# Three hand-overs between engines in a two-layer encoder step: weight low parts to VectorE, output scaling to ScalarE and GpSimd, one chunk normalised tile by tile

## The chip, the cores and the metric

The kernel runs on one core of a Trainium2 chip. A core has five engines that run their own instruction streams in order: TensorE (PE; its weight loads are shown apart as PEld), VectorE (DVE), ScalarE (ACT), GpSimd (POOL) and SyncE (SP), whose queue issues nearly all DMAs here. They wait for one another by semaphores. The metric is device microseconds of one execution, the median over the timed runs. The profile is one more execution, recorded by the hardware profiler.

## The reference, cut to what matters

The reference is one inference step of a two-layer encoder: 2048 prompt frames and one chunk of 64 sample frames with caches, model width 1024, all in fp32. Each layer is

```python
xn = _rms(h, pre_g)
...                                   # projections of xn @ w_in, gated attention of the layer
return h + _rms((o * jax.nn.silu(g)) @ w_out, post_g), state

def _rms(x, g):
    y = xf * lax.rsqrt(jnp.mean(xf * xf, axis=-1, keepdims=True) + RMS_EPS)
    return (y * g).astype(x.dtype)
```

Layer 0 has two groups of heads (latent attention over all earlier chunks, and a band of nine chunks with a learned bias), layer 1 a sliding window of three chunks with grouped queries (16 query heads, 2 key heads) and attention sinks. The new cache rows are outputs too.

## The kernel before, in words

All matrix products are made to fp32 accuracy out of fp32r products: an operand is split into a high part (fp32 rounded to fp32r by a copy on ScalarE) and a low part (the fp32 value minus the high part), and three products of high and low parts are added up in PSUM (`mm3`, L231). So nearly every operand costs a copy on ScalarE and a subtraction on another engine. Tiles that come out of PSUM get their low part on DVE (`lo_of`, L213); a few that lie in SBUF get it on POOL: the projection weights (`load_w`, L228), the gated attention output (L1749 in phase 5, L1268 in phase 3).

The work stands in five phases. In the trace, phase 1 (projections of layer 0) runs to about 715 us, phase 2 (latent attention) to about 1345, phase 3 (band attention and layer 0's W_out) to about 1850, phase 4 (projections of layer 1) from about 1805 to 2270, and phase 5 (window attention and layer 1's W_out) from there to the end.

*Weights and inputs (phases 1 and 4).* `load_w` (L216) brings a block of projection columns in pieces of up to 1024 columns: a DMA into a raw buffer R, the high part by ScalarE (L227), the low part by POOL (L228). `norm_chunk` (L243) brings up to three tiles of 128 tokens into the same raw buffers (there are five in phase 1), squares and sums each on ScalarE (L255), makes the reciprocal root of the mean on DVE by three Newton steps of tiny operations (`rstd_of`, L180: for the three tiles together, 128x3, unless `start` is given, as it is for the very first chunk, where each tile has its own chain on 128x1), scales the tile by it and by the row of gains (L263), and transposes it on PE (L267) into X. A 128x1 chain takes three DVE operations for a Newton step (L195 to L197), a 128x3 chain four (L192, L193, L196, L197).

*W_out and its tail (phases 3 and 5).* `out_proj` (L966) multiplies the split MM of 128 tokens with W_out in two halves of 512 columns, evicts them to z, and sums their squares on ScalarE (L982). Its `tail` then makes the reciprocal root on POOL and DVE, scales z by it and by the gains on DVE (L994, two halves of 512), adds the residual x on POOL (L1002) and sends the rows out. The very last tile (`J.last`) does all on DVE and in halves.

*Phase 5's steady part.* A block is 128 queries and 4 units (2 key heads by 2 parities). A unit scores on PE (L1684), adds the mask and takes maxima on DVE (L1687, L1688), adds the sink on POOL (L1689), exponentiates on ScalarE (L1696), sums on POOL (L1700), turns on PE (L1705) and splits P into PT (L211 on ScalarE, L214 on DVE), multiplies with V on PE (L1712), and writes its part of OT on DVE (L1802). OT has two buffers, taken in turn. After four units the `gate` (L1714) scales OT by the sums (L1736), multiplies it with the gate G on POOL (L1742), and splits it into MM (high L211 on ScalarE, low L1749 on POOL), which is free for W_out afterwards. W_out's products and tails of earlier blocks are spread between these steps by a pump.

*What sets the order.* A scheduler of the framework orders the instructions of each engine by simulated times. In phase 3 and in phase 5 after the first steps it is switched off for PE, DVE, ScalarE and SP: there the order is that in which the code issues. POOL's order is the scheduler's throughout.

Of the kernel before, what the change touches and what calls it, by code (L numbers as in the profile page):

```python
# [10 lines left out]
AF = mybir.ActivationFunctionType  # L11
ALU = mybir.AluOpType
# [4 lines left out]
SEQ, DS, PAST, DM = 2048, 64, 1024, 1024  # L17
# [45 lines left out]
HALVES4 = [HALVES[1], HALVES[0]]  # L63
# [47 lines left out]
def kernel(ctx, tc, a, o, upto=5):  # L111

    nc = tc.nc
    S = K()
    dma = nc.sync.dma_start
# [25 lines left out]
    sH = scratch("sH", [T, 1024])  # L141
# [74 lines left out]
    def load_w(pw, raw, src, kt, w, slot):  # L216

        W = pw.tile([128, slot], F32R, name="W")
        Wv = W[:, :2 * kt * w].rearrange("p (a k c) -> p a k c", a=2, k=kt)
        sv = src.rearrange("(k p) c -> p k c", p=128)  # L220
        step = max(1, 1024 // w)
        for k0 in range(0, kt, step):
            k1 = min(kt, k0 + step)
            R = raw.tile([128, 1024], F32, name="R")
            Rv = R[:, :(k1 - k0) * w].rearrange("p (k c) -> p k c", c=w)
            dma(Rv, sv[:, k0:k1])
            nc.scalar.activation(Wv[:, 0, k0:k1], Rv, AF.Copy)  # L227
            nc.gpsimd.tensor_tensor(Wv[:, 1, k0:k1], Rv, Wv[:, 0, k0:k1], op=ALU.subtract)  # L228
        return Wv

    def mm3(ps, lhs, rhs, kt):  # L231
# [8 lines left out]
    def prompt_or_sample(t0, r):  # L240
        return a["x_prompt"][t0:t0 + r] if t0 < SEQ else a["x_sample"]

    def norm_chunk(px, raw, xin, pt, src, g_pre, c0, n, start=None):  # L243

        X = px.tile([128, 2, KT, 384], F32R, name="X")
        tiles = tok_tiles(c0, n)
        ss = xin.tile([128, 3], F32, name="ss3")
        if tiles[-1][2] < 128:
            nc.gpsimd.memset(ss, 1.0)
        xs = []  # L250
        for i, (t0, off, r) in enumerate(tiles):
            x = raw.tile([128, 1024], F32, name="R")
            dma(x[:r], src(t0, r))
            sq = xin.tile([128, DM], mybir.dt.bfloat16, name="sq", bufs=1)
            nc.scalar.activation(sq[:r], x[:r], AF.Square, accum_out=ss[:r, i:i + 1])  # L255
            xs.append(x)
            if start and i == 0:
                start()
        y = None if start else rstd_of(ss[:, :len(tiles)], 128, DM)
        for i, (t0, off, r) in enumerate(tiles):  # L260
            x = xs[i]
            yi = rstd_of(ss[:, i:i + 1], 128, DM) if start else y[:, i:i + 1]
            nc.vector.scalar_tensor_tensor(x[:r], x[:r], yi[:r], g_pre[:r], op0=ALU.mult, op1=ALU.mult)  # L263
            for k0 in range(0, KT, 4):
                p = pt.tile([128, 4, 128], F32, name="pt")
                for k in range(4):
                    nc.tensor.transpose(p[:, k, :r], x[:r, (k0 + k) * 128:(k0 + k + 1) * 128], ident[:r, :r])  # L267
                hi = X[:, 0, k0:k0 + 4, off:off + r]
                copy(hi, p[:, :, :r])
                lo_of(X[:, 1, k0:k0 + 4, off:off + r], p[:, :, :r], hi)  # L270
        return X
# [694 lines left out]
    def out_proj(J, wk, zp, M, W, t0, r, res, g_post, put):  # L966
# [3 lines left out]
        z = z0 or zp.tile([128, DM], F32, name="z", bufs=2)  # L970
        ss = small.tile([128, 2], F32, name="ss2")
# [12 lines left out]
        def tail():  # L984
            eng = nc.vector if J.last else nc.gpsimd
            eng.tensor_tensor(ss[:r, 0:1], ss[:r, 0:1], ss[:r, 1:2], op=ALU.add)
            y = rstd_of(ss[:r, 0:1], r, DM, eng)
            if not J.last:
                yield
                yield  # L990
                yield
            for c in range(2):
                cs = slice(c * 512, c * 512 + 512)
                nc.vector.scalar_tensor_tensor(z[:r, cs], z[:r, cs], y, g_post[:r, cs], op0=ALU.mult, op1=ALU.mult)  # L994
                if J.last:
                    eng.tensor_tensor(res[:r, cs], z[:r, cs], res[:r, cs], op=ALU.add)
                    dma(put(t0, r)[:, cs], res[:r, cs])
                elif c == 0:
                    yield
            if J.last:  # L1000
                return
            nc.gpsimd.tensor_tensor(res[:r], z[:r], res[:r], op=ALU.add)  # L1002
            for _ in range(1 + DPUT):
                yield
            J.put(put(t0, r), res[:r])
# [30 lines left out]
    def jobs(banks):  # L1036
        J = K()
        J.loaded, J.ready, J.made, J.done, J.banks, J.n, J.credit = False, [], 0, 0, banks, 0, 0.0
        J.last, J.put = False, dma
        J.early, J.half, J.n_early, J.MM = [], {}, 0, {}  # L1040
        J.side, J.tails, J.load, J.samp = Fill(), Fill(), Fill(), Fill()

# [418 lines left out]
    def phase4():  # L1461

        with ExitStack() as st, ExitStack() as st_m:
            pool, pool_m = pools(st, "left"), pools(st_m, "left")
            px0, pw0 = pool("px4", 1), pool("pw4", 1)
            raw, rows, xin = pool_m("raw4", 6), pool_m("rows4", 1), pool_m("xin4", 2)
            px, pw = Ring(px0), Ring(pw0)
# [72 lines left out]
            Xs4 = {}  # L1540

            def build(c):
                Xs4[c] = norm_chunk(px, raw, xin, pt, lambda t0, r: sH[t0:t0 + r], g_pre, *c)

            def weights(col, specs):
                w = 256 if specs == ["kv"] else 128 * len(specs)
# [28 lines left out]
                            yield  # L1575
                put()

            build(HALVES4[0][0])
            W = weights(*pieces[0][0])
            yield  # L1580
            keep = ctx.enter_context(tc.tile_pool(name="keep", bufs=1, side="right", reuse_waits="tile"))
# [64 lines left out]
    def phase5():  # L1646

        with ExitStack() as st:
# [4 lines left out]
            ps_o, ps_p = pool("ps_o5", 1, space=PSUM), pool("ps_p5", 1, space=PSUM)  # L1653
            J = jobs([(ps_p, "proj")])
            J.open = 0
            J.mm = None
            mask = one.tile([128, 256], F32, name="mask")
            nc.gpsimd.memset(mask, 0.0)
            nc.gpsimd.memset(mask[0:64, 192:256], NEG)
# [366 lines left out]
```

## Time and profile before

| what | value |
|---|---|
| three timed runs | 2733.17, 2735.3, 2743.01 us; median 2735.3 |
| the profiled execution | 2728.45 us, its span 2726.7, mean granted TensorE clock 0.985 |
| PE / PEld busy | 94% / 86% of the span |
| DVE / ACT / POOL busy | 54% / 51% / 28% |
| DMA | 437.92 MB, 161 GB/s over the span |

Lines of the timeline and of the groups give the start, the duration in us, engine, line, operation, out<-in and shapes; behind them, in brackets, the idle time of the engine just ahead and who ended it. A row with x2 or more stands for several instructions that follow each other. Lines of waits give the total in us, the number of times, and the longest.

### The profile page before, as it was taken

What the parts mean: (1) busy time and instruction counts of PE and PEld (TensorE: products, weight loads), DVE (VectorE), ACT (ScalarE), POOL (GpSimd) and SP (SyncE); (2) the same over time, 40 slices, a digit from 0 to 9 for tenths busy, and PEclk for the clock granted to TensorE, in tenths of its full rate; (3) what the DMA queues carried; (4) which work ended last, traced back from release to release, by engine and by line L of the source; (5) the groups of instructions that cost most, each with busy time, mean ns of one, the idle gap of its engine ahead of it and who ended that gap; (6) DMA issues with size and microseconds to landing.
All of it is one profiled execution on the core that took longest, in us unless ns stands there. A gap on an engine that the chain in (4) does not pass through costs nothing.

```text
span 2726.7 us, 46699 instructions
## 1 busy us (share of the span) xinstructions
PE 2565.9 (94%) x16296; PEld 2340.5 (86%) x16296; DVE 1471.5 (54%) x4050; ACT 1392.1 (51%) x3548; POOL 772.6 (28%) x1312
## 2 busy tenths in 40 slices
PE   6999999999999999999999999989999999999997
PEld 6999999899998888888777878769999998787886
DVE  5542235352127878787667666545113104787884
ACT  4332232333237777777666665552233224777783
POOL 2123122113112323321101323553113220344444
PEclk9999999999999999999899999999999999999999
DMA  6456443737537666661477676756525429455551
GB/s 236 160 155 213 124 150 97 249 110 228 165 95 210 183 180 188 170 165 55 169 202 187 179 187 172 205 187 216 155 99 166 128 70 250 109 139 134 136 132 70
DMA packets 382283, 437.92 MB, mean 161 GB/s; under 512 B 49937, under 2 KB 308889, under 8 KB 378817
## 3 DMA queue, kind: packets, MB, share of 16 engines
q1 hardware_dynamic: 382048, 434.95, 54.4%
q8 instruction: 129, 2.11, 0.3%
q14 instruction: 106, 0.86, 0.1%
HBM read 282.80 MB, written 157.09 MB: 161 GB/s over the span
## 4 chain that ended last, share of the span: by engine, by line
PE 73%; DVE 10%; ACT 6%; DMA 5%; issue 3%; POOL 2%; SPq 0%; ACTq 0%; DVEq 0%; POOLq 0%
PE pm L237 37%; PE proj L963 10%; PE s L682 6%; PE acc L753 4%; PE t L725 3%; DVE PT L214 2%; PE acc L1215 2%; PE t L1705 2%; PE acc L1712 2%; PE s L1175 2%; PE t L1202 1%; PE s L1684 1%; ACT P L701 1%; DVE m L688 1%; ACT PT L211 1%
## 5 line engine op out<-in xcount | busy, mean ns | idle before, releaser
L237 PE MATMUL pm<-X,W 128*128 128x384 f32 (+2 forms) x4536 | 753.4, 325 | 2.4 <-DVE ev L214 0.9
L237 PEld LDWEIGHTS pm<-X,W 128*128 128x128 f32 x4536 | 732.5, 190 | 5.5 <-DVE ev L214 1.1
L211 ACT ACTIVATE PT<-t 128x512 fp32r<-128x512 f32 (+3 forms) x704 | 344.6, 505 | 272.0 <-PE t L1202 120.4
L214 DVE SCALAR_TENSOR_TENSOR PT<-t,PT 128x512 fp32r<-128x512 f32 (+3 forms) x688 | 375.5, 569 | 105.2 <-ACT PT L211 103.4
L963 PE MATMUL proj<-Wo,MM 128*128 128x512 f32 (+1 forms) x1464 | 404.0, 406 | 18.1 <-ACT z L211 14.7
L228 POOL TENSOR_TENSOR W<-R,W 128x768 fp32r<-128x768 f32 (+3 forms) x114 | 230.4, 2048 | 534.0 <-ACT W L227 533.7
L214 DVE SCALAR_TENSOR_TENSOR ev<-pm,ev 128x256 fp32r<-128x256 f32 (+3 forms) x197 | 98.7, 503 | 467.3 <-ACT ev L1552 169.3
L963 PEld LDWEIGHTS proj<-Wo,MM 128*128 128x128 f32 (+1 forms) x1464 | 252.2, 186 | 68.8 <-ACT z L211 20.1
L237 PE MATMUL pm<-W,X 128*128 128x256 f32 (+5 forms) x2040 | 281.2, 297 | 0.0
L237 PEld LDWEIGHTS pm<-W,X 128*128 128x128 f32 (+1 forms) x2040 | 271.6, 187 | 1.4 <-POOL W L228 0.3
L701 ACT ACTIVATE P<-s,m 128x512 f32<-128x512 f32 (+9 forms) x344 | 209.5, 616 | 32.8 <-DVE m L690 30.5
L682 PE MATMUL s<-KA,Q 128*128 128x512 f32 (+7 forms) x640 | 201.1, 396 | 9.7 <-ACT P L701 8.8
L725 PE MATMUL t<-ident,P 128*128 128x128 f32 x1088 | 176.3, 276 | 3.4 <-ACT P L701 0.8
L688 DVE TENSOR_REDUCE m<-s 128x1 f32<-128x480 f32 (+7 forms) x216 | 132.4, 613 | 79.1 <-PE s L682 78.7
L725 PEld LDWEIGHTS t<-ident,P 128*128 128x128 f32 x1088 | 134.7, 141 | 41.5 <-ACT P L701 14.9
L753 PE MATMUL acc<-PT,V 128*128 128x256 f32 x1152 | 155.9, 285 | 6.6 <-DVE OT L762 6.6
L753 PEld LDWEIGHTS acc<-PT,V 128*128 128x128 f32 x1152 | 140.3, 188 | 12.0 <-PE t L725 6.0
L1696 ACT ACTIVATE P<-s,m 128x256 f32<-128x256 f32 (+2 forms) x264 | 119.7, 466 | 11.6 <-DVE m L1688 10.3
L1687 DVE CUSTOM_DVE_ANT_0 s<-s,mask 128x256 f32<-128x256 f32 (+1 forms) x256 | 107.7, 422 | 19.0 <-PE t L1705 8.1
L682 PE MATMUL s<-KR,Q 128*128 128x384 f32 (+6 forms) x320 | 116.3, 363 | 0.7 <-DMA Q<-sQR 0.7
L227 ACT ACTIVATE W<-R 128x768 fp32r<-128x768 f32 (+3 forms) x114 | 98.2, 910 | 36.5 <-DMA R<-in_ab_w_in_dram 18.2
L1179 DVE CUSTOM_DVE_ANT_0 s<-s,bias 128x640 f32<-128x640 f32 (+4 forms) x128 | 95.2, 744 | 38.6 <-PE s L1175 37.3
(249 smaller groups left out, 3961.0 us busy)
## 6 DMA issues: line engine op xcount, KB each, us to landing
Q<-sQA SPq DMA_DIRECT2D x128, 128.0 KB, 3.4
sWO<-W SPq DMA_DIRECT2D x32, 512.0 KB, 3.9
Q<-sQB SPq DMA_DIRECT2D x128, 128.0 KB, 3.5
Wo<-sWO SPq DMA_DIRECT2D x16, 1024.0 KB, 8.4
Q<-sQC SPq DMA_DIRECT2D x32, 512.0 KB, 7.6
R<-in_ab_w_in_dram SPq DMA_DIRECT2D x40, 384.0 KB, 3.5
K<-sKB SPq DMA_DIRECT2D x56, 256.0 KB, 5.0
V<-sVB SPq DMA_DIRECT2D x24, 512.0 KB, 6.2
```

The costliest lines, as they stand in the source:

```text
L211: nc.scalar.activation(out, in_, AF.Copy)
L214: nc.vector.scalar_tensor_tensor(out, x, scale, hi, op0=ALU.mult, op1=ALU.subtract)
L228: nc.gpsimd.tensor_tensor(Wv[:, 1, k0:k1], Rv, Wv[:, 0, k0:k1], op=ALU.subtract)
L237: nc.tensor.matmul(ps, lhs(x, k), rhs(y, k), start=(j == 0), stop=(j == n - 1))
L682: nc.tensor.matmul(s[:r, :n], self.Q[:, x, self.qo:self.qo + r], rhs, start=(x == 0), stop=(x == 2))
L688: nc.vector.tensor_reduce(m[:r, j:j + 1], s[:r, :n], axis=AX.X, op=ALU.max)
L701: nc.scalar.activation(self.P[:r, o0:o0 + n], self.s.pop(j)[:r, :n], AF.Exp, bias=self.m[:r, 6:7], accum_out=acc)
L725: nc.tensor.transpose(t[:, b], self.P[:, (b0 + b) * 128:(b0 + b + 1) * 128], ident)
L753: nc.tensor.matmul(acc[:, (i // 2) % 2], H.V[:, b0 + b], PT[:, x, b], start=(b0 + b == 0 and x == 0), stop=(b0 + b == i and x == 1))
L963: nc.tensor.matmul(p, M[:, x, k, :r], W[k][:, y, cs], start=(k == k0 and t == 0), stop=(k == k1 - 1 and t == 2))
L1687: nc.vector.tensor_tensor_reduce(s[:, c, :w], s[:, c, :w], mk, 1.0, -3e38, ALU.add, ALU.max, m[:, 0, c:c + 1])
L1696: nc.scalar.activation(self.P[:, c, :w], self.s[:, c, :w], AF.Exp, bias=m[:, 1, c:c + 1], accum_out=m[:, 0, c:c + 1])
```

## The change

It does three things.

1. `load_w`: the low part of a piece of projection weights is subtracted on DVE and not on POOL.
2. `norm_chunk` gets a flag `single`: each tile has its own chain for the reciprocal root, as the very first chunk has. It is set for the first chunk of layer 1 (tokens 1024 to 1407).
3. Phase 5 sets `J.scale`. Where it is set and the tile isn't the last of all, ScalarE multiplies the whole z (1024 columns) by the reciprocal root, the tail yields once, and POOL multiplies by the row of gains; the two DVE operations fall away there. Fifteen of the 17 tiles of phase 5 take this way; the last two keep the DVE form.

```diff
@@ load_w
-            nc.gpsimd.tensor_tensor(Wv[:, 1, k0:k1], Rv, Wv[:, 0, k0:k1], op=ALU.subtract)
+            nc.vector.tensor_tensor(Wv[:, 1, k0:k1], Rv, Wv[:, 0, k0:k1], op=ALU.subtract)
@@ norm_chunk
-    def norm_chunk(px, raw, xin, pt, src, g_pre, c0, n, start=None):
+    def norm_chunk(px, raw, xin, pt, src, g_pre, c0, n, start=None, single=False):
...
-        y = None if start else rstd_of(ss[:, :len(tiles)], 128, DM)
+        single = single or start
+        y = None if single else rstd_of(ss[:, :len(tiles)], 128, DM)
...
-            yi = rstd_of(ss[:, i:i + 1], 128, DM) if start else y[:, i:i + 1]
+            yi = rstd_of(ss[:, i:i + 1], 128, DM) if single else y[:, i:i + 1]
@@ out_proj, tail
-            for c in range(2):
+            if J.scale and not J.last:
+                nc.scalar.activation(z[:r], z[:r], AF.Copy, scale=y)
+                yield
+                nc.gpsimd.tensor_tensor(z[:r], z[:r], g_post[:r], op=ALU.mult)
+            for c in range(0 if J.last or not J.scale else 2, 2):
@@ jobs
-        J.last, J.put = False, dma
+        J.last, J.put, J.scale = False, dma, False
@@ phase4
-            def build(c):
-                Xs4[c] = norm_chunk(px, raw, xin, pt, lambda t0, r: sH[t0:t0 + r], g_pre, *c)
+            def build(c, single=False):
+                Xs4[c] = norm_chunk(px, raw, xin, pt, lambda t0, r: sH[t0:t0 + r], g_pre, *c, single=single)
...
-            build(HALVES4[0][0])
+            build(HALVES4[0][0], True)
@@ phase5
-            J.mm = None
+            J.mm, J.scale = None, True
```

Behind the edits the line numbers grow by up to five: L263 becomes L264, L994 L999 (L994 is then ScalarE's scaling, L996 POOL's product), L1002 L1007, L1742 L1747, L1749 L1754, L1802 L1807.

How the order moves shows best in one regular block of phase 5. POOL first, before; OT is the block's output, G its gate, MM the split operand, z and x the tile of W_out whose tail falls into this block:

```order
L1742 TENSOR_TENSOR OT_29039<-OT_29039,G_29396 128x1024
L1700 TENSOR_TENSOR rsum_28987<-m_29502 128x4
L1689 TENSOR_TENSOR m_29569<-m_29569,sink_25775 128x4
L1749 TENSOR_TENSOR MM_29629<-OT_29039,MM_29629 128x1024
L1002 TENSOR_TENSOR x_29149<-z_29151,x_29149 128x1024
L1700 TENSOR_TENSOR rsum_28987<-m_29569 128x4
```

POOL in the same block now:

```order
L1747 TENSOR_TENSOR OT_29062<-OT_29062,G_29419 128x1024
L1705 TENSOR_TENSOR rsum_29010<-m_29525 128x4
L1694 TENSOR_TENSOR m_29592<-m_29592,sink_25798 128x4
L996 TENSOR_TENSOR z_29174<-z_29174,g_post_21578 128x1024
L1754 TENSOR_TENSOR MM_29652<-OT_29062,MM_29652 128x1024
L1007 TENSOR_TENSOR x_29172<-z_29174,x_29172 128x1024
L1705 TENSOR_TENSOR rsum_29010<-m_29592 128x4
```

The product with the gains (L996) has come ahead of MM's low part (L1754). It stands so in 11 successive blocks; in one of these the residual add (L1002) stood ahead of L1749 before. In the block ahead of them L996, the gate's product and the add all stand ahead of the low part, and in the last but one block L1754 stands ahead of L996.

ScalarE in this block, before (PT is the split P, tbm a part of the unit's output on its way to OT):

```order
L982 ACTIVATE sq_29454,ss2_29453<-z_29452 128x512
L211 ACTIVATE PT_29619<-t_29614 128x512
L211 ACTIVATE MM_29629<-OT_29039 128x1024
L211 ACTIVATE tbm_29642<-acc_29609 64x512
L1696 ACTIVATE P_29645,m_29569<-s_29568,m_29569 128x256 x4
```

and now:

```order
L983 ACTIVATE sq_29477,ss2_29476<-z_29475 128x512
L211 ACTIVATE PT_29642<-t_29637 128x512
L994 ACTIVATE z_29174<-z_29174,rs_29427 128x1024
L211 ACTIVATE MM_29652<-OT_29062 128x1024
L211 ACTIVATE tbm_29665<-acc_29632 64x512
L1701 ACTIVATE P_29668,m_29592<-s_29591,m_29592 128x256 x4
```

The scaling of z stands between PT and MM's high part, and the unit's exponentials follow behind all three.

DVE where layer 1's first chunk is normalised, before (R are the three tiles, rs the reciprocal roots, X the transposed chunk):

```order
L196 TENSOR_SCALAR rs_21175<-rs_21175 128x3
L197 TENSOR_TENSOR rs_21175<-rs_21175 128x3
L263 SCALAR_TENSOR_TENSOR R_21163<-R_21163,rs_21175,g_pre_21154 128x1024
L263 SCALAR_TENSOR_TENSOR R_21167<-R_21167,rs_21175,g_pre_21154 128x1024
L263 SCALAR_TENSOR_TENSOR R_21171<-R_21171,rs_21175,g_pre_21154 128x1024
L214 SCALAR_TENSOR_TENSOR X_21161<-pt_21192,X_21161 128x4x128
```

and now, from the end of the first tile's chain:

```order
L197 TENSOR_TENSOR rs_21175<-rs_21175 128x1
L197 TENSOR_TENSOR rs_21203<-rs_21203 128x1
L186 TENSOR_SCALAR rs_21231<-ss3_21162 128x1
L264 SCALAR_TENSOR_TENSOR R_21163<-R_21163,rs_21175,g_pre_21154 128x1024
L195 SCALAR_TENSOR_TENSOR rs_21203<-rs_21203 128x1
L187 TENSOR_SCALAR rs_21231<-rs_21231 128x1
L187 TENSOR_SCALAR rs_21316<-rs_21316 128x1
L228 TENSOR_TENSOR W_21259<-R_21260,W_21259 128x768
L196 TENSOR_SCALAR rs_21203<-rs_21203 128x1
```

The first tile is scaled as soon as its own chain is through; the chains of the other two and the low parts of the weights (L228) are woven in behind it.

PE's instructions stand in the same order in phases 2, 3 and 5 of both kernels; in phases 1 and 4 the scheduler has placed some of them anew.

## The prediction

> **What bounds the kernel now.** I read the page's head first: busy shares, then the chain that ended last.
>
> ```profile
> span 2726.7 us, 46699 instructions
> PE 2565.9 (94%) x16296; PEld 2340.5 (86%) x16296; DVE 1471.5 (54%) x4050; ACT 1392.1 (51%) x3548; POOL 772.6 (28%) x1312
> PE 73%; DVE 10%; ACT 6%; DMA 5%; issue 3%; POOL 2%; SPq 0%; ACTq 0%; DVEq 0%; POOLq 0%
> ```
>
> TensorE is busy for 2565.9 of 2726.7 us. No part of the change touches a matmul, so time can only come from or go into the 160.8 us in which PE stands. Next the windows, one row for a stage that the change touches (second number: its length; third: PE busy, then PEld, DVE, ACT, POOL, the granted clock, DMA share, GB/s).
>
> ```profile
> 0.00:60.00 60.00, 37.41 (x206) 34.81 (x207) 29.60 (x114) 26.91 (x49) 14.47 (x13) 0.91 0.77 261
> 60.00:390.00 330.00, 325.36 (x2162) 319.23 (x2162) 128.25 (x412) 102.44 (x216) 75.92 (x50) 1.00 0.48 154
> 390.00:720.00 330.00, 318.77 (x1933) 305.41 (x1932) 130.11 (x427) 106.31 (x259) 74.39 (x61) 0.98 0.56 178
> 1800.00:1870.00 70.00, 55.30 (x278) 49.00 (x277) 44.74 (x107) 33.70 (x61) 35.37 (x61) 0.90 0.67 224
> 1870.00:2270.00 400.00, 399.63 (x2637) 398.52 (x2636) 80.33 (x261) 106.27 (x216) 98.92 (x75) 1.00 0.45 137
> 2330.00:2670.00 340.00, 325.07 (x1876) 273.08 (x1874) 283.13 (x754) 263.51 (x791) 152.99 (x335) 0.99 0.50 125
> ```
>
> PE idles 22.6 us in the start, 4.6 and 11.2 in the rest of phase 1, 14.7 at the boundary of phases 3 and 4, 0.4 in phase 4, and 14.9 in phase 5's steady part. The second question is who is waited for there; the answer is a different one in each stage, so each edit is read from its own stage.
>
> **Edit 1, weight lows from POOL to DVE.** It takes 114 instructions off POOL; the page's group, five rows of the timeline and three of PE's waits:
>
> ```profile
> L228 POOL TENSOR_TENSOR W<-R,W 128x768 fp32r<-128x768 f32 (+3 forms) x114 | 230.4, 2048 | 534.0 <-ACT W L227 533.7
> 11.39 3.57 POOL L228 TENSOR_TENSOR W<-R,W 128x768 fp32r<-128x768 f32 x2 [10.94 <-ACT W L227]
> 11.50 1.71 DVE L195 SCALAR_TENSOR_TENSOR rs<-rs 128x1 f32<-128x1 f32 x1
> 13.31 1.65 DVE L195 SCALAR_TENSOR_TENSOR rs<-rs 128x1 f32<-128x1 f32 x1
> 17.23 1.28 DVE L263 SCALAR_TENSOR_TENSOR R<-R,rs,g_pre 128x1024 f32<-128x1024 f32 x1
> 105.45 2.41 DVE L197 TENSOR_TENSOR rs<-rs 128x1 f32<-128x1 f32 x1
> PE pt L354 <- DVE c L368: 2.5, 2, 1.6
> PE pt L354 <- DVE c L368: 2.9, 1, 2.9
> PE po L388 <- POOL k L380: 3.1, 1, 3.1
> ```
>
> DVE has no line L228, so its price there is an estimate: DVE's two-SBUF-input operation of 1024 columns took 1.28 us (L263), so about 0.95 us for 768 columns by proportion, some 120 us in all against 230.4 on POOL. What this buys is not POOL's time, which PE hardly waits for, but an end to the stalls of tiny DVE operations: L195, on one column, took 1.71 and 1.65 us beside POOL's two L228 from 11.39 on, and L197 2.41 us at 105.45, where DVE was otherwise free. These chains lead to c L368, for which PE waited 2.5 us before 390 and 2.9 after (the two rows, one window each). I count 4 of these 5.4 us as gone. At the start, PE's 3.1 us for POOL's k L380 and the raw buffers' release come earlier by 1 to 3 us. That is 6 us for phase 1. Bounds: at best all 8.5 us of these three rows and the 3.4 us of two held operations at the start, -12; at worst evictions queue behind an L228 that waits for ScalarE's high part ahead of them in DVE's in-order queue, three of them for one 0.95 us each, +3. I take -6, near the middle of what the rows name. In phase 4 PE is busy for 399.63 of 400 us and DVE for 80.33: some 40 more DVE us hide under PE; 0, and ±1.
>
> [...]
>
> **Edit 2, layer 1's first chunk tile by tile.** The boundary, by timeline:
>
> ```profile
> 1805.10 1.69 DVE L196 TENSOR_SCALAR rs<-rs 128x3 f32<-128x3 f32 x1
> 1813.25 3.68 DVE L263 SCALAR_TENSOR_TENSOR R<-R,rs,g_pre 128x1024 f32<-128x1024 f32 x3
> 1814.59 3.67 PE L267 MATMUL pt<-ident,R 128*128 128x128 f32 x16 [9.81 <-DVE R L263]
> 1817.37 2.38 POOL L1268 TENSOR_TENSOR MM<-M,MM 128x1024 fp32r<-128x1024 f32 x1 [3.89 <-ACT MM L211]
> 1829.95 1.06 ACT L211 ACTIVATE MM<-M 128x1024 fp32r<-128x1024 f32 x1 [0.29 <-DMA M<-sMB]
> 1833.51 0.73 PE L963 MATMUL proj<-Wo,MM 128*128 128x512 f32 x2 [1.26 <-POOL MM L1268]
> ```
>
> The chain of the three tiles' rstd is held by POOL's L228 as in phase 1, and R is normalised at 1813.25. With edit 1 gone from POOL and one tile's chain instead of three, I put the first tile near 1804.1, so PE's 9.81 us hole is filled from its start. But only 24 transposes fill it; what follows is W_out's last product, which needs POOL's L1268 (1817.37 + 2.38) and later an M that a DMA brings for 1829.95. MM's copy follows the transposes in ScalarE's queue and moves up by little over 1 us, since its M's DMA now stands behind the chunk's loads on SP; PE's last wait, at 1833.51, follows at the DMA's pace. By hand that is -3 us. Bounds: -6, if the M loads move up with the transposes, and +2, if they don't and sit behind the loads.
>
> **Edit 3, phase 5's scaling from DVE to ScalarE and GpSimd.** PE's and DVE's waits of 2330 to 2670, then one regular block of 128 queries by timeline:
>
> ```profile
> PE acc L1712 <- DVE OT L1802: 11.3, 12, 3.8
> DVE OT L1802 <- POOL MM L1749: 9.4, 3, 4.8
> 2542.23 2.40 POOL L1742 TENSOR_TENSOR OT<-OT,G 128x1024 f32<-128x1024 f32 x1 [4.17 <-DVE OT L1736]
> 2546.31 2.65 POOL L1749 TENSOR_TENSOR MM<-OT,MM 128x1024 fp32r<-128x1024 f32 x1 [1.37 <-ACT MM L211]
> 2544.69 0.60 ACT L211 ACTIVATE PT<-t 128x512 fp32r<-128x512 f32 x1 [0.93 <-PE t L1705]
> 2545.19 1.05 ACT L211 ACTIVATE MM<-OT 128x1024 fp32r<-128x1024 f32 x1
> 2545.93 3.58 DVE L994 SCALAR_TENSOR_TENSOR z<-z,rs,g_post 128x512 f32<-128x512 f32 x2
> 2549.43 0.67 DVE L1802 TENSOR_TENSOR OT<-acc,tbm 64x512 f32<-64x512 f32 x1
> 2550.25 1.17 PE L1712 MATMUL acc<-PT,VC 128*128 128x512 f32 x4 [0.74 <-DVE OT L1802]
> ```
>
> Of PE's 14.9 idle us, 11.3 are this one wait, once a block. L1802 writes the first rows of a new OT; OT has two buffers, so it must come after POOL's L1749 (MM low), the last reader of the OT before the previous one. Here L1749 ends at 2548.96 and the second L994 at 2549.51, and L1802 follows at once. What goes: 2 x L994 on DVE, after which L1802 could start at L1749's end. What comes: one ScalarE pass over 1024 columns, 1.05 us by the row of MM's copy (same shape), and one POOL product of 1024 columns, 2.40 us by L1742's row (same shape and kind). Their place decides. In the order of the changed kernel ScalarE does z between PT and MM's high part, and POOL does the product ahead of L1754 (L1749's new number) in 11 regular blocks. So: z scaled 2545.19 to 2546.25; POOL's product to 2548.67; MM's low part, 2.40 us where no DVE operation interferes, to about 2551.05; L1807 (the old L1802) there, against 2549.43: 1.6 us later, and PE with it. The high part, 1.05 us later, hides under POOL's product. One of the 11 blocks had another order before; for the other ten 10 x 1.6 = +16.0. That one and two more places:
>
> ```profile
> 2497.29 2.37 POOL L1002 TENSOR_TENSOR x<-z,x 128x1024 f32<-128x1024 f32 x1 [1.72 <-DVE z L994]
> 2499.62 2.35 POOL L1749 TENSOR_TENSOR MM<-OT,MM 128x1024 fp32r<-128x1024 f32 x1
> 2502.00 0.68 DVE L1802 TENSOR_TENSOR OT<-acc,tbm 64x512 f32<-64x512 f32 x1 [4.79 <-POOL MM L1749]
> 2502.74 1.22 PE L1712 MATMUL acc<-PT,VC 128*128 128x512 f32 x2 [3.80 <-DVE OT L1802]
> 2403.20 0.68 DVE L1802 TENSOR_TENSOR OT<-acc,tbm 64x512 f32<-64x512 f32 x1 [2.30 <-POOL MM L1749]
> 2693.96 2.36 PE L963 MATMUL proj<-Wo,MM 128*128 128x512 f32 x9 [1.48 <-POOL MM L1749]
> ```
>
> The block at 2497 is the precedent: POOL's residual add (2.37 us) happened to stand ahead of L1749, and PE waited 3.80 instead of about 0.7 us. There the new order puts the product, ready sooner than the add was, ahead of L1749, which then ends near 2500.1 and not at 2501.97: -1.9 in place of +1.6. In the block at 2403 three POOL operations of 2.4 us now precede the low part, where it was one: +2.5. At 2693.96 the low part now precedes the product, so the 1.48 us go: -1.5. Phase 5: 16.0 - 1.9 + 2.5 - 1.5 = +15.1. Bounds: +7, if the new order costs half of 1.6 a block, and +23, if tiny DVE operations before the next exponentials are held by the residual add for 0.8 us a block besides.
>
> [...]
>
> **Sum.** -6 - 3 + 0 + 15.1 = +6.1 us. The profiled execution took 2728.45 us (its span and 1.75 us around it), 6.85 below the median 2735.3 of the three timed runs; it would become 2734.6, and the median 2741.4.
>
> **Rivals.**
> A, phase 5 gains: the two L994 were what L1802 waited for, POOL's product is cheaper or overlaps the low part, and L1802 starts when tbm is there. For it: in the quoted block L994 ended last, 0.55 us after L1749. Against it: POOL takes its work in order, and the 4.79 us row shows L1802 waiting for POOL with DVE free. At most the 11.3 us and the 1.5 at the tail go: -13 - 9 = -22, 2713.
> B, slower: the low parts on DVE sit in front of PSUM evictions in phase 1. For it: DVE is 40% busy there and its queue is in order, and an L228 there waits for a DMA and for ScalarE. Against it: PE has only 4.6 us of holes in 60 to 390. It decides from about ten evictions held for 0.95 us each: +3 instead of -6, with the 15.1 of phase 5 and the +2 of the boundary's bad end +20, 2755.
> C, nothing to be measured: POOL's freed time and phase 5's new wait cancel, within ±3 us of 2735. This lies inside my own case's range.
>
> **How the numbers follow.** A measurement of this kernel can tell about 0.5%, 13.7 us: below 2721.6 is faster, above 2749.0 slower. Chances: my case 0.70, A 0.12, B 0.18. My case by its bounds goes from -6 - 3 + 7 = -2 at the light end of edit 3 to -6 - 3 + 23 = +14 at the heavy one, and to -8 if phase 1 gives its 12 besides the light end. Faster is A and a sliver, 0.13. Slower is most of B, 0.16, and the upper end of my case, 0.09, together 0.25; the rest, 0.62, is the same. The range leaves out A and what lies above B: -11 to +20, 2724 to 2755.
>
> **What would show it.** Right: in a regular block of phase 5 POOL's rows read product, low part, residual add, each about 2.4 us, and PE's wait for L1807 grows from 0.7 to about 2.4 us, some 29 us in all where it was 11.3; the steady part's PE idle grows from 14.9 to about 32. Before 720, no DVE operation of one column over 0.5 us beside a weight low, and PE's waits for L368 and L380 gone. At the boundary, transposes from about 1805.5 and the last wait some 3 us sooner. Wrong: a phase 5 wait that shrinks (A), or PE waiting on PSUM evictions (ev, X) behind L228 (B).

## The result and the profile after

The changed kernel takes 2749.51 us (median of 7 runs, 2747.19 to 2755.96); the kernel before, run beside it, 2735.3 (7 runs, 2732.37 to 2743.01). The ratio is 1.0050, 95% interval 1.0035 to 1.0065: slower by 14.2 us where 6.1 were forecast. That is just past the 13.7 us that the prediction drew as its line, by the median alone: the interval reaches from 9.6 to 17.8 us. The two profiled executions lie 21.0 us apart in span (2726.7 and 2747.7); the one of before was among the fastest of its kernel. The places below are read from these two traces, and the sizes are checked against timed runs in the experiments.

The page after, the three lines that answer to those shown of before:

```profile
span 2747.7 us, 46656 instructions
PE 2577.8 (94%) x16296; PEld 2350.8 (86%) x16296; DVE 1508.9 (55%) x4155; ACT 1405.8 (51%) x3563; POOL 578.1 (21%) x1213
PE 71%; DVE 9%; ACT 6%; DMA 5%; POOL 5%; issue 4%; SPq 1%; ACTq 0%; POOLq 0%; DVEq 0%
```

POOL works 194.5 us less and yet holds 5% of the chain where it was 2%. And PE is busy 11.9 us longer with the same 16296 matmuls: some of them have become slower, for which the prediction had no term. The windows of after (second number the length, third PE busy; behind POOL's column the granted clock):

```profile
0.00:60.00 60.00, 39.83 (x216) 36.37 (x217) 35.39 (x140) 26.96 (x48) 0.74 (x6) 0.94 0.76 262
60.00:390.00 330.00, 327.39 (x2171) 322.26 (x2170) 147.72 (x427) 103.69 (x219) 14.76 (x19) 0.99 0.49 157
390.00:720.00 330.00, 323.08 (x2007) 309.72 (x2007) 143.87 (x460) 108.75 (x264) 17.56 (x31) 0.99 0.56 179
1870.00:2270.00 400.00, 399.62 (x2643) 398.71 (x2642) 112.93 (x301) 106.97 (x216) 19.95 (x34) 1.00 0.45 139
2350.00:2690.00 340.00, 309.15 (x1710) 262.26 (x1708) 228.84 (x668) 253.42 (x743) 170.12 (x335) 0.95 0.47 116
```

Phase 1 is fuller, phase 4 as full as it was; phase 5's steady part has 30.9 us without PE work and a clock of 0.95, where it was 14.9 us and 0.99. When a stage's work ends is read from the first and last starts of its matmuls. Here are, of before and then of after, the last transposes of phase 1, the scores of phase 3's band attention, and the scores of phase 5:

```profile
L502 PE MATMUL po<-ident,ev x20: 270/272/476, 630.3 to 711.6; 128*128 128x128 f32 x16, 128*64 128x128 f32 x4
L1175 PE MATMUL s<-K,Q x448: 220/309/637, 1331.8 to 1778.6; 128*128 128x320 f32 x128, 128*128 128x512 f32 x6, 128*128 128x128 f32 x6, 128*128 128x384 f32 x5
L1684 PE MATMUL s<-KC,Q x512: 221/283/582, 2276.3 to 2662.3; 128*128 128x256 f32 x161, 128*128 128x128 f32 x10
```

```profile
L503 PE MATMUL po<-ident,ev x20: 270/272/330, 620.9 to 700.6; 128*128 128x128 f32 x16, 128*64 128x128 f32 x4
L1180 PE MATMUL s<-K,Q x448: 220/309/636, 1321.5 to 1771.5; 128*128 128x320 f32 x128, 128*128 128x512 f32 x6, 128*128 128x128 f32 x6, 128*128 128x384 f32 x5
L1689 PE MATMUL s<-KC,Q x512: 221/283/562, 2267.8 to 2680.6; 128*128 128x256 f32 x161, 128*128 128x128 f32 x10
```

The lead over before is 11.0 us at the end of phase 1 (711.6 against 700.6), 7.1 at the end of phase 3's scores, 8.5 at phase 5's first score; at its last score the changed kernel is 18.3 behind, at the end 21.0. So phase 1 gained 11.0, phases 2 and 3 gave 3.9 of it back, the boundary and phase 4 gained 1.4, and phase 5 lost 29.5. Of the 3.9, 2.2 are a wait that PE had not in phase 3 before, for keys that a DMA brings (L1180, K<-sKB, once); the rest isn't followed up.

One regular block of phase 5 of after, by timeline:

```profile
2548.69 1.14 ACT L994 ACTIVATE z<-z,rs 128x1024 f32<-128x1024 f32 x1
2549.73 1.05 ACT L211 ACTIVATE MM<-OT 128x1024 fp32r<-128x1024 f32 x1
2549.91 2.39 POOL L996 TENSOR_TENSOR z<-z,g_post 128x1024 f32<-128x1024 f32 x1 [1.45 <-ACT z L994]
2552.26 2.37 POOL L1754 TENSOR_TENSOR MM<-OT,MM 128x1024 fp32r<-128x1024 f32 x1
2554.58 2.36 POOL L1007 TENSOR_TENSOR x<-z,x 128x1024 f32<-128x1024 f32 x1
2554.66 0.68 DVE L1807 TENSOR_TENSOR OT<-acc,tbm 64x512 f32<-64x512 f32 x1 [5.14 <-POOL MM L1754]
2555.49 2.01 PE L1717 MATMUL acc<-PT,VC 128*128 128x512 f32 x4 [2.46 <-DVE OT L1807]
```

This is the chain that was forecast, link by link: scaling, product 2.39, low part 2.37, then OT, and PE waits 2.46 us where it was 0.74. The total from 2330 to the end, after and then before:

```profile
PE acc L1717 <- DVE OT L1807: 30.6, 12, 3.4
```

```profile
PE acc L1712 <- DVE OT L1802: 13.1, 14, 3.8
```

That is +17.5 us. But the PE row of the block has a second number to read, its duration: four matmuls of 512 columns took 2.01 us, where the same four took 1.17 before. The same row of the blocks on either side:

```profile
2529.40 1.16 PE L1717 MATMUL acc<-PT,VC 128*128 128x512 f32 x4 [2.47 <-DVE OT L1807]
2582.84 2.04 PE L1717 MATMUL acc<-PT,VC 128*128 128x512 f32 x4 [2.51 <-DVE OT L1807]
```

And the windows around two such holes, two rows for the one that ends at 2529.40 and three for the one that ends at 2555.49 (the third number from the right is the granted clock; why the windows are 3.41 us long is said below):

```profile
2524.82:2528.24 3.42, 2.11 (x16) 1.63 (x14) 0.00 (x0) 3.40 (x12) 3.42 (x2) 1.00 1.09 222
2528.24:2531.65 3.41, 2.25 (x15) 2.06 (x16) 2.94 (x11) 0.70 (x3) 2.94 (x4) 1.00 0.02 6
2552.12:2555.54 3.42, 0.96 (x7) 0.52 (x4) 0.88 (x2) 2.31 (x9) 3.42 (x3) 1.00 0.72 159
2555.54:2558.95 3.41, 3.41 (x12) 2.92 (x13) 2.44 (x10) 0.56 (x2) 1.76 (x3) 0.50 0.33 136
2558.95:2562.36 3.41, 3.41 (x21) 2.96 (x20) 2.66 (x9) 3.37 (x11) 1.10 (x6) 1.00 0.45 154
```

Behind the hole that ends at 2555.49 the granted clock is 0.50 for 3.41 us, then 1.00 again; behind the equally long one that ends at 2529.40 it stays 1.00. That gives both prices from the same trace: the block from 2529.40 to 2555.49 lasted 26.09 us with a long hole at full clock, the next, to 2582.84, 27.35 with the same hole and the lowered clock. Before, a block took 24.35. The wait costs 1.74 us, the clock another 1.26. Ten of the twelve holes were followed by the low clock, which makes 10 x 1.2 = 12 us beside the 17.5 of waits. That these two add up to exactly 29.5 is chance. Over the whole of phase 5, before and then after:

```profile
2276.30:2726.70 450.40, 408.94 (x2313) 340.58 (x2312) 341.42 (x927) 316.42 (x943) 188.52 (x411) 0.98 0.50 132
2267.80:2747.70 479.90, 422.77 (x2313) 352.59 (x2311) 303.73 (x897) 329.96 (x958) 218.13 (x426) 0.95 0.48 124
```

PE stood 15.7 us longer and was busy 13.8 us longer with the same 2313 matmuls; the longer waits for OT are in part made up for by shorter ones elsewhere.

What sets one hole apart from an equally long one can be looked for in the traces too. In the traces of before and after the granted clock is either 1.00 or 0.50. Every stretch at 0.50 (14 before, 25 after) lasts 3.41 us or a whole multiple of that, and within each trace all of them begin a whole number of 3.41 us apart (the end of the execution cuts the last one short). In each of these two traces they so lie on a grid of 3.41 us. The hole that ends at 2555.49 lies inside one stretch of the grid, in which PE is busy for 0.96 of 3.42 us, a share of 0.28; the one that ends at 2529.40 lies across a border and leaves PE busy for 0.62 and 0.66 of two stretches.

In the steady part of phase 5 of these two traces (stretches that begin between 2330 and 2690 us), the low clock followed each of the twelve stretches of which PE was busy for 0.39 or less, and none of the other 199, of which PE was busy for 0.51 or more. This bound isn't general: in the changed kernel the stretch from 2292.72 to 2296.13 was 0.64 busy, and the low clock followed. A block with the low clock lasts 27.3 us, which is eight stretches, so the next hole comes at the same place of the grid (the low clocks from 2398.52 to 2480.44 us begin 27.31 us apart), and the ten holes are no ten independent trials. No run moved the holes against the grid on purpose; this part is read, not tested.

### The profile page after: what moved, and what is told of

It is laid out like the page before. It is cut to its first block, busy times and chain, and to the rows that moved or that the text cites. A ratio compares the mean times of both kernels' runs of the same rounds, so it can differ in the third digit from the quotient of the medians.

```text
span 2747.7 us, 46656 instructions
## 1 busy us (share of the span) xinstructions
PE 2577.8 (94%) x16296; PEld 2350.8 (86%) x16296; DVE 1508.9 (55%) x4155; ACT 1405.8 (51%) x3563; POOL 578.1 (21%) x1213
## 4 chain that ended last, share of the span: by engine, by line
PE 71%; DVE 9%; ACT 6%; DMA 5%; POOL 5%; issue 4%; SPq 1%; ACTq 0%; POOLq 0%; DVEq 0%
PE pm L237 37%; PE proj L964 7%; PE s L683 6%; PE acc L754 4%; PE t L726 3%; PE acc L1220 2%; PE acc L1717 2%; DVE PT L214 2%; PE s L1180 2%; PE t L1207 1%; PE t L1710 1%; POOL MM L1754 1%; PE s L1689 1%; ACT P L702 1%; DVE m L689 1%
## 5 line engine op out<-in xcount | busy, mean ns | idle before, releaser
L964 PE MATMUL proj<-Wo,MM 128*128 128x512 f32 (+1 forms) x1464 | 406.7, 408 | 15.1 <-ACT z L211 14.7
L228 DVE TENSOR_TENSOR W<-R,W 128x768 fp32r<-128x768 f32 (+3 forms) x114 | 118.1, 1073 | 133.0 <-ACT W L227 132.7
L726 PEld LDWEIGHTS t<-ident,P 128*128 128x128 f32 x1088 | 134.6, 141 | 41.8 <-ACT P L702 15.1
```

The source lines that it names most:

```text
L228: nc.vector.tensor_tensor(Wv[:, 1, k0:k1], Rv, Wv[:, 0, k0:k1], op=ALU.subtract)
L726: nc.tensor.transpose(t[:, b], self.P[:, (b0 + b) * 128:(b0 + b + 1) * 128], ident)
L964: nc.tensor.matmul(p, M[:, x, k, :r], W[k][:, y, cs], start=(k == k0 and t == 0), stop=(k == k1 - 1 and t == 2))
```

## The experiments

The theory: phase 5 loses because POOL's product stands ahead of MM's low part and OT's reuse waits for that; PE's hole costs its length, and a lowered clock on top. The rivals: ScalarE's extra pass delays the exponentials; phase 5 suffers from what the earlier phases do to it; the parts hang together. Ratios are to the kernel before, run on the same chip.

**Without the third part.**

```diff
-            J.mm, J.scale = None, True
+            J.mm, J.scale = None, False
```

> The changed kernel without its third part: phase 5 scales z on VectorE in two halves as before; the weight lows on VectorE and the single-tile chains stay. Theory (phase 5 loses because POOL's product stands ahead of MM's low part): phase 5 is as before, block period 24.3 us and PE's wait for OT about 0.7 us a block, while phase 5 still starts 8 to 9 us earlier, so about 2727 us. Rival (phase 5's loss comes from what the earlier phases do to it, a shifted DMA or clock phase): the long blocks stay, about 2748 us.

Measured: 2719.53 us, ratio 0.9952 (0.9933 to 0.9972), 12.3 us less than before. Phase 5 starts at 2268.2 us and its blocks are of the old kind:

```profile
2542.09 1.17 PE L1717 MATMUL acc<-PT,VC 128*128 128x512 f32 x4 [0.72 <-DVE OT L1807]
```

The first two parts are a gain, a larger one than forecast, and phase 5's loss belongs to the third part alone. The time is 7.5 us below the 2727 of the expectation. Half of that is the kernel before, which ran at 2731.85 on this chip and not at 2735.3; the other half is that the timed gain is 12.3 us, where the two traces had given 8.5 at phase 5's start.

**The third part alone.**

```diff
-            nc.vector.tensor_tensor(Wv[:, 1, k0:k1], Rv, Wv[:, 0, k0:k1], op=ALU.subtract)
+            nc.gpsimd.tensor_tensor(Wv[:, 1, k0:k1], Rv, Wv[:, 0, k0:k1], op=ALU.subtract)
...
-            build(HALVES4[0][0], True)
+            build(HALVES4[0][0])
```

> The kernel before with the third part alone. Theory: blocks of 27.3 us from the same wait, nothing gained before phase 5, so 2735 + 29 = about 2764 us. Rival (the parts hang together): phase 5 shorter than in the changed kernel, 2750 us or less.

Measured: 2760.33 us, ratio 1.0104 (1.0077 to 1.0130), +28.5 us, with blocks of 27.3 us. The parts add up: -12.3 and +28.5 are +16.2, against the +14.2 of the whole change.

**Three buffers for OT.**

```diff
-                G = qp.tile([128, 8, 128], F32, name="G")
+                G = qp.tile([128, 8, 128], F32, name="G", bufs=1)
...
-                        B.OT = ot.tile([128, 8, 128], F32, name="OT", bufs=2)
+                        B.OT = ot.tile([128, 8, 128], F32, name="OT", bufs=3)
```

> The changed kernel with three buffers for OT instead of two (and one instead of two for the gate G, to make room): the first write of a block's OT no longer waits for POOL, and POOL's and ScalarE's orders stay. Theory (POOL's order is the cause, by that wait): PE's wait for OT goes to under 0.4 us a block, the clock stays full, block period 23.6 to 24.0 us, about 2712 to 2718 us. Rival (ScalarE's extra pass of 1.05 us delays the exponentials and PE's turns behind them): a wait of about 1 us a block moves to the turns, period 24.5 us or more, 2727 us or more.

Measured: 2704.41 us, ratio 0.9891 (0.9873 to 0.9910), 27.4 us faster than before and better still than expected. POOL's order is that of the changed kernel, and PE's wait is gone. The waits and the window from 2330 to 2650:

```profile
PE acc L1717 <- DVE OT L1807: 0.2, 1, 0.2
```

```profile
2330.00:2650.00 320.00, 315.98 (x1831) 266.29 (x1830) 245.53 (x713) 268.28 (x779) 175.87 (x342) 1.00 0.53 133
```

The first product of a block, twice in succession:

```profile
2513.26 1.09 PE L1717 MATMUL acc<-PT,VC 128*128 128x512 f32 x4
2536.88 1.09 PE L1717 MATMUL acc<-PT,VC 128*128 128x512 f32 x4
```

The block takes 23.62 us, and ScalarE's extra pass, which is still made, costs PE no wait: that rival is out. The place on POOL hurts only through OT's reuse. This is the best version found.

**MM first, scaling behind it.**

```diff
             if J.scale and not J.last:
+                yield
+                yield
                 nc.scalar.activation(z[:r], z[:r], AF.Copy, scale=y)
```

> The changed kernel with two more yields ahead of ScalarE's scaling of z in the tail: ScalarE then makes MM's high part first and scales z behind it, and POOL makes MM's low part ahead of the product. Buffers as in the change. Theory (place on POOL decides): the low part ends as early as before, no VectorE operation stands between it and OT, PE's wait for OT 0.3 to 0.7 us a block, no slow matmuls; 2720 to 2727 us. Rival (ScalarE's extra pass): the pass still precedes the exponentials, so a wait of about 1 us a block, 2732 us or more.

Measured: 2738.03 us, ratio 1.0019 (1.0007 to 1.0031). The theory's number was missed and the rival's was met, so the trace had to tell which is true. POOL does the low part first, OT is written in time, and PE's old wait is gone; but a new one stands a few steps later:

```profile
2548.02 2.36 POOL L1009 TENSOR_TENSOR x<-z,x 128x1024 f32<-128x1024 f32 x1
2548.28 2.12 DVE L1695 SCALAR_TENSOR_TENSOR m<-m,nsink 128x4 f32<-128x4 f32 x1
2550.33 1.27 DVE L214 SCALAR_TENSOR_TENSOR PT<-t,PT 128x512 fp32r<-128x512 f32 x2
2551.06 0.66 PE L1712 MATMUL t<-ident,P 128*128 128x128 f32 x4 [2.08 <-DVE PT L214]
```

The window behind that wait:

```profile
2553.00:2555.00 2.00, 2.00 (x6) 1.53 (x5) 1.86 (x10) 0.45 (x1) 1.51 (x9) 0.50 0.49 80
```

A VectorE operation on four columns took 2.12 us beside POOL's residual add, whose end it shares to 0.02 us; the split of PT stands behind it, PE waits 2.08 us for that, and the clock falls to 0.50. Not ScalarE's pass, but the same hold of VectorE by POOL that the prediction had read in phase 1, and had priced at up to 0.8 us a block in phase 5's upper bound.

**The same without the residual add.**

```diff
-            nc.gpsimd.tensor_tensor(res[:r], z[:r], res[:r], op=ALU.add)
+            if not J.scale:
+                nc.gpsimd.tensor_tensor(res[:r], z[:r], res[:r], op=ALU.add)
```

> The run with the late scaling, and besides it phase 5 leaves out the residual add of layer 1 on the 15 tiles that take the new way (their outputs are then the residual alone). Theory (there POOL's residual add holds VectorE's maximum L1695, four columns, for 2.1 us, and so the split of PT, PE's turns and the clock): without the add that operation takes about 0.2 us, PE's wait of 2.1 us a block goes, blocks of 23.6 to 24.2 us, a single time of 2700 to 2712 us. Rival (the wait comes from ScalarE's later exponentials or from VectorE's own queue): the 2 us stay at PE's turns, blocks of 27 us, 2730 us or more.

Measured: 2707.09 us, a single run. The operation on four columns (now L1696) takes its 0.16 us again, and the regular blocks have no hole:

```profile
2513.08 0.16 DVE L1696 SCALAR_TENSOR_TENSOR m<-m,nsink 128x4 f32<-128x4 f32 x1
```

So the add was what held it, and the miss of the run before is explained: moving the product behind the low part puts the add where VectorE needs to get through.

**Half of the third part.**

```diff
-                nc.scalar.activation(z[:r], z[:r], AF.Copy, scale=y)
+                nc.scalar.activation(z[:r, 512:], z[:r, 512:], AF.Copy, scale=y)
+                nc.vector.scalar_tensor_tensor(z[:r, :512], z[:r, :512], y, g_post[:r, :512], op0=ALU.mult, op1=ALU.mult)
                 yield
-                nc.gpsimd.tensor_tensor(z[:r], z[:r], g_post[:r], op=ALU.mult)
+                nc.gpsimd.tensor_tensor(z[:r, 512:], z[:r, 512:], g_post[:r, 512:], op=ALU.mult)
```

> The changed kernel with half of the third part: of each z ScalarE and POOL do columns 512 to 1023, VectorE the other half in one operation as before. POOL's order stays (product, low part, residual add), but the product is 512 columns, 1.27 us by the row of that shape in the run before, ScalarE's pass 0.6. Theory with a threshold (the delay in POOL's order is first eaten by the time in which the old kernel waited for its second VectorE half, and the clock falls only behind a long hole): MM's low part ends about where VectorE's second half ended, PE's wait for OT 0.7 to 1.1 us a block, clock full, blocks of 24.3 to 24.7 us, 2719 to 2726 us. Rival (the loss goes with the amount moved, and half of it half as much): blocks of 25.8 us, about 2734 us.

Measured: 2725.59 us, ratio 0.9977 (0.9966 to 0.9987), in time as the threshold theory said, at the upper end of its range. The block and its wait were longer than the theory had them: 25.16 us, with a hole of 1.53.

```profile
2538.29 0.75 DVE L995 SCALAR_TENSOR_TENSOR z<-z,rs,g_post 128x512 f32<-128x512 f32 x1
2538.34 1.86 POOL L997 TENSOR_TENSOR z<-z,g_post 128x512 f32<-128x512 f32 x1 [1.04 <-ACT z L994]
2543.41 1.16 PE L1718 MATMUL acc<-PT,VC 128*128 128x512 f32 x4 [1.53 <-DVE OT L1808]
```

The product took 1.86 us and not 1.27: here VectorE came first, at 2538.29, and POOL was the one held. Behind 1.53 us of hole the matmuls take 1.16, at full clock, so the block is longer by the hole alone (24.35 + 0.8). The loss is not in proportion: half of the moved columns cost 0.8 us a block over the old one, all of them 3.0.

**PE kept busy in the hole.**

```diff
                 def av(self):
+                    if (self.g, self.e) == (0, 1) and J.made > 2:
+                        d = ps_t.tile([128, 512], F32, name="t")
+                        for _ in range(5):
+                            nc.tensor.matmul(d, self.B.VC[:, 0, 0], self.tasks[0][:, 0], start=True, stop=True)
```

> The changed kernel with five more matmuls of 512 columns in each of 12 blocks of phase 5, on a PSUM buffer that nobody reads: they stand on PE just ahead of the product that waits for OT, and need nothing that is late. At 0.39 us each they fill 2.0 of the 2.5 us hole and don't move what PE waits for. Theory (the wait costs 1.75 us a block, and a lowered clock behind the long hole another 1.2): the granted clock stays full, the four products behind the hole take 1.16 instead of 2.04 us, blocks of 26.1 instead of 27.3 us, so about 12 us less than the changed kernel, 1.001 of the time before (2737 us against 2735), although PE does more. Rival (those matmuls are slow for another reason, such as POOL's and the DMAs' traffic at that moment): 2.0 us as before, blocks of 27.3 us or more, 1.005 or more.

Measured: 2737.01 us, ratio 1.0018 (1.0006 to 1.0029), where the changed kernel had 1.0050: with 65 more matmuls (there are thirteen such blocks, not twelve) it is some 9 us faster than without. The five took 1.32 us together and not the 2.0 expected, and so fill half of the hole. One block, and the window of the steady part:

```profile
2575.71 1.32 PE L1796 MATMUL t<-PT,VC 128*128 128x512 f32 x5
2578.28 1.20 PE L1717 MATMUL acc<-PT,VC 128*128 128x512 f32 x4 [1.25 <-DVE OT L1811]
```

```profile
2340.00:2680.00 340.00, 322.95 (x1848) 272.32 (x1847) 238.45 (x698) 264.28 (x771) 172.97 (x340) 1.00 0.49 124
```

OT comes no earlier, PE still stands for 1.25 us, but the clock is 1.00 throughout and the four products take 1.20. So the slow matmuls came from the idle hole: POOL's product, low part and add run around it as in the changed kernel. Of the change's loss 9 us by these ratios, and 12 by the blocks of the trace, are the clock's.

**The old scaling with three buffers for OT.**

```diff
-            J.mm, J.scale = None, True
+            J.mm, J.scale = None, False
...
-                        B.OT = ot.tile([128, 8, 128], F32, name="OT", bufs=2)
+                        B.OT = ot.tile([128, 8, 128], F32, name="OT", bufs=3)
```

The gate G has one buffer here too.

> The weight lows on VectorE and the single-tile chains, phase 5's scaling on VectorE as before, and three buffers for OT with one for the gate G. Tells what the third part is worth once OT's reuse waits no more for POOL. Theory: VectorE's second half of the scaling, which stands ahead of OT's first write in its queue, is still held by POOL's low part, so PE's wait of about 0.7 us a block stays: 2717 to 2721 us, and the third part gains some 15 us in the run with three buffers. Rival (the wait was OT's reuse all along, and scaling on VectorE costs nothing): 2702 to 2707 us.

Measured: 2715.3 us, ratio 0.9935 (0.9919 to 0.9950); a little under the expectation, with the wait as it said:

```profile
2534.66 3.57 DVE L999 SCALAR_TENSOR_TENSOR z<-z,rs,g_post 128x512 f32<-128x512 f32 x2
2535.04 2.64 POOL L1754 TENSOR_TENSOR MM<-OT,MM 128x1024 fp32r<-128x1024 f32 x1 [1.35 <-ACT MM L211]
2538.97 1.17 PE L1717 MATMUL acc<-PT,VC 128*128 128x512 f32 x4 [0.72 <-DVE OT L1807]
```

OT waits for POOL no more, but VectorE's second half of the scaling does, and it stands ahead of OT's write in VectorE's queue. With three buffers the third part is worth 2715.3 - 2704.4 = 10.9 us (12 by the two ratios, each against the kernel before on its own chip): what the change wanted to remove was a real cost, and having only two buffers of OT kept it from paying.

**The first part alone, and the second alone.** Against the changed kernel, the first:

```diff
-            build(HALVES4[0][0], True)
+            build(HALVES4[0][0])
...
-            J.mm, J.scale = None, True
+            J.mm, J.scale = None, False
```

> The kernel before with the first part alone, weight lows on VectorE. Theory: it carries most of the 12 us that the first two parts gave together, all of phase 1's 10 us and a few at the boundary, since POOL's holds of VectorE's chains go with it: 2721 to 2725 us. Rival (the single-tile chains carry the boundary, and the weight lows alone stall there, behind a chain of three tiles): 2726 us or more.

Measured for the first: 2721.92 us, ratio 0.9959 (0.9941 to 0.9977), 8.8 us less than the 2730.68 of before on that chip, as its theory had it. The second:

```diff
-            nc.vector.tensor_tensor(Wv[:, 1, k0:k1], Rv, Wv[:, 0, k0:k1], op=ALU.subtract)
+            nc.gpsimd.tensor_tensor(Wv[:, 1, k0:k1], Rv, Wv[:, 0, k0:k1], op=ALU.subtract)
...
-            J.mm, J.scale = None, True
+            J.mm, J.scale = None, False
```

> The kernel before with the second part alone: layer 1's first chunk normalised tile by tile, weight lows still on POOL. Theory (the hold of VectorE's tiny operations by POOL's weight lows is what delays the boundary, and the parts need each other): with the lows still on POOL the first tile's own chain is held too, so that little is gained, -2 to +1 us, and the 12 us of both parts are nearly all the first part's. Rival (one tile's chain is short enough to get through between the lows): 4 us or more gained at the boundary.

Measured for the second: 2733.39 us, ratio 0.9997 (0.9981 to 1.0012): nothing, as its theory had it in time. The theory's detail was wrong: the first tile's chain is not held, and that tile is scaled at 1805.30 where it was 1813.25. The second and third tiles' chains still have long operations (an L195 on one column took 1.77 us at 1806.50, where 0.22 is usual); that POOL's weight lows hold them, as in the trace of before, is an inference. Whether the second part adds anything to the first stays open: 0.9952 and 0.9959 have overlapping intervals, and the traces differ by 3.3 us at phase 5's first score (2268.2 against 2271.5).

## Why the prediction was right or wrong

- *The total.* +14.2 us lies in the stated range of -11 to +20, and that is in part luck. The prediction's own case ended at +14; the range reached to +20 for rival B, which did not happen. And the first two parts gained 12.3 us in timed runs where 9 were forecast, which hid a part of what phase 5 lost beyond its bounds. By the prediction's own line of 2749.0 the kernel is slower, to which it gave a chance of 0.25.
- *The sign, and rival A.* Slower, through the named link: POOL's product, MM's low part, OT's write, PE. The wait of the regular block came out as 2.46 us against the 2.4 announced, the block at 2497 changed by -1.7 us (3.80 to 2.07) against -1.9, the one at 2403 by +2.2 (0.57 to 2.81) against +2.5. Rival A, a shrinking wait, did not happen; with three buffers for OT it does.
- *Phase 5's size, the step that failed.* The term was +15.1 us, bounds +7 to +23; the trace shows +29.5. The step "1.6 us later, and PE with it" took PE's work behind the hole as unchanged. It was not: the clock halves behind ten of twelve holes, some 1.2 us each, and PE is busy 13.8 us longer in phase 5. The waits alone, +17.5 us, lie within the bounds. The sign of it stood in the very row that the prediction quoted as its precedent: behind the 3.80 us hole at 2502.74 two matmuls took 1.22 us, as long as four took at 2550.25. The prediction read the wait in brackets and not the duration beside it. The trace of before, read again there:

```profile
2502.60:2504.60 2.00, 1.86 (x6) 1.68 (x7) 1.90 (x9) 0.61 (x2) 0.00 (x0) 0.50 0.03 10
```

  In the trace of after, holes of 2.46 to 3.38 us were followed by the lower clock in ten blocks, and so was a gap of 2.08 in the run with the late scaling; one of 1.53 in the run with half of the part was not. The length of the gap alone doesn't decide here, since the one of 2.47 us at 2529.40 was not followed by it either: what differed was how much of one 3.41 us stretch the gap took up, as read above.
- *The product on GpSimd.* It took 2.39 us, as the row of the same shape (2.40) had it.
- *Phase 1.* Forecast -6, bounds -12 to +3; the traces show -11.0 at its end, near the better bound. VectorE's tiny operations are free: L195's longest, the third of the three durations in ns, was 1768 before 390 us and is 298 now. Before:

```profile
L195 DVE SCALAR_TENSOR_TENSOR rs<-rs x57: 206/219/1768, 5.8 to 201.4; 128x1 f32<-128x1 f32 x57
```

  And after:

```profile
L195 DVE SCALAR_TENSOR_TENSOR rs<-rs x57: 197/219/298, 6.0 to 195.2; 128x1 f32<-128x1 f32 x57
```

  The weight low took about 0.95 us on VectorE for 768 columns, as estimated (mean 0.99). Of the three waits that were to go, the two for c are gone, and of the one for k 1.7 of 3.1 us are left. A hold of POOL by a weight low on VectorE is there too, but small: at the start of phase 4 POOL's L192 on one column took 0.85 us at 1799.94, beside VectorE's L228 from 1799.77, where 0.19 is usual. Rival B is out: PE's waits for evictions (ev) before 720 us come to 6.7 us, against 6.1 before, and phase 1 got shorter. The 3.9 us that phases 2 and 3 gave back were not foreseen.
- *The boundary.* Forecast -3, bounds -6 to +2; from the last score of phase 3 to the first of phase 5 the traces differ by -1.4. The first tile came early as announced, but then:

```profile
1804.58 1.41 DVE L999 SCALAR_TENSOR_TENSOR z<-z,rs,g_post 128x512 f32<-128x512 f32 x2 [1.07 <-POOL rs L197]
1805.97 1.28 DVE L264 SCALAR_TENSOR_TENSOR R<-R,rs,g_pre 128x1024 f32<-128x1024 f32 x1
1806.08 3.40 POOL L1007 TENSOR_TENSOR x<-z,x 128x1024 f32<-128x1024 f32 x1 [0.54 <-DVE rs L187]
1807.23 3.06 DVE L228 TENSOR_TENSOR W<-R,W 128x768 fp32r<-128x768 f32 x1
1807.31 1.97 PE L268 MATMUL pt<-ident,R 128*128 128x128 f32 x8 [7.61 <-DVE rs L196]
```

  The second tile's scaling (1805.97) stands in VectorE's queue behind W_out's z, which waits for POOL; PE stood 7.61 us between the first tile and the second. A wait took the place of the one removed, and the weight low (3.06 us beside POOL's add) is now held itself.

## What to carry to other kernels

An operation that is moved to an engine with time to spare lands in that engine's order: ask what stands behind it there and which buffer's reuse waits for that, and give the buffer before you move the work (the same move cost 28 us with two buffers of OT and gained 11 with three). Here that was one more OT, with one G less to make room. When a wait of TensorE grows, read the duration of the matmuls behind holes of that length in the trace you have, not only the hole, and the granted clock in short windows. And an elementwise pass on GpSimd also held VectorE's small operations here (2.12 us in place of 0.16); when two orders are to choose from, look at which of them puts such a pass beside the critical small one.

## What the runs showed of the hardware that was not expected

- The granted clock of TensorE fell to 0.50 for 3.41 us, or a multiple, in the traces of before and after, each time a whole number of 3.41 us from the other times in the same trace. In after, holes of 2.46 to 3.38 us were followed by it in ten of twelve blocks, and holes of 2.47 and 2.07 us that lay across a border of this grid were not; in the run with the late scaling a gap of 2.08 us was, in the run with half of the part one of 1.53 us was not. In phase 5's steady part of the two traces it followed every stretch of the grid of which PE was busy for 0.39 or less, and none with 0.51 or more. Sixty-five useless matmuls in the gaps made the kernel some 9 us faster.
- A hold between VectorE and GpSimd was seen both ways: POOL's 512-column product took 1.86 us when VectorE had started 0.05 us before it (a product of that shape took 1.27 at 2327.0 in the trace of before), VectorE's four-column operation 2.12 us when POOL had started 0.26 us before (0.16 without POOL's add). In these rows whoever came second waited.
